# The last projection of the second row block by seven half-size products, with weight sums read back from memory

## The chip, the cores and the metric

One Trainium2 chip, one core. The time is the device time of one execution in microseconds; of a kernel that runs several times the median is given. Its five queues work side by side: TensorE (matmuls, PE in the profile), VectorE (DVE), ScalarE (ACT), GpSimd (POOL) and the sync queue (SP), which only issues DMAs. All DMAs share 16 engines.

## The reference

Two sequences of 512 and 1024 rows with 1024 columns pass through one layer: a mixer (attention and gated linear attention) and then an MLP, each added to its input, and a last norm. The change is in the MLP alone; all is float32.

```python
D_FF = -(-8 * D_MODEL // (3 * 256)) * 256        # 2816
def swiglu(hn, w_gate, w_up, w_down):
    return (jax.nn.silu(hn @ w_gate) * (hn @ w_up)) @ w_down
...
    x = x + swiglu(rmsnorm(x, norm2_g[l]), w_gate[l], w_up[l], w_down[l])
return rmsnorm(x, final_norm_g)
```

## The kernel before

The mixer's result goes to memory (`x2d`). The MLP then takes the 1536 rows as two blocks of 768 rows (`Block`, 6 tiles of 128 rows), and for each block all 2816 inner columns in 11 groups of 256 (`Group`; `NG` is 11). A product of two float32 matrices is made of three matmuls: each operand is split into a high part and the rest (`split`: ScalarE casts the high part, VectorE subtracts), and high x high, high x rest and rest x high are added in PSUM.

Gate and up are made with Winograd's form of Strassen's scheme. A block's normed rows, transposed, are cut in quarters (upper and lower half of the 1024 inner indices, even and odd tiles of rows), and from them seven forms (`FORMS`, b11 to b22, t1 to t4) are kept for the whole block, high and rest (`self.B`). A group's 1024 x 256 weights are cut in quarters as well, and `Weights.prepare(n)` makes seven sums of them, one for each product n, with four additions on VectorE, and splits each into a tile cw (pools `wc`, 5 buffers, and `hx`, 2). `Group.product(wn, n)` then multiplies cw with form n: 4 x 3 matmuls of 384 columns (L1075) into a PSUM tile gu; `common` combines the seven results (L1080, L1083). `w_gate` applies silu, `w_up` multiplies and splits the factor into g.

`Group.down(i)` multiplies g with the rows of `w_down` of the group (tile wd, L84 to L86) in the plain way: for each of 6 row tiles and each half of the 1024 output columns 2 x 3 matmuls of 512 columns, then an addition on VectorE into the result `xa` (L1142). After the last group `final` norms the rows and stores them.

The list `units` sets the order of a group: seven gate products, the down steps of the group before it, seven up products. `raw` loads the weights of one group, 1 MB a load, on the sync queue (tile rw or rd, pool `wr`, 2 buffers); `prepare_to` makes weights four products ahead of their use in the source. The framework then orders each engine's instructions by itself, by what is ready. During block 0, groups 3, 5 and 7, `blocks[1].rows` and `blocks[1].turn` norm and transpose the rows of block 1; `put` splits each form into a wc tile (f) and stores both halves in memory (`formd`), and `Block.fetch` loads them while block 0 ends. `blocks[1].residual` loads block 1's rows into `xa` at its first gate product.

Of the kernel before, what the change touches and what calls it, by code (L numbers as in the profile page):

```python
# [8 lines left out]
F32 = mybir.dt.float32  # L9
F32R = mybir.dt.float32r  # L10
# [33 lines left out]
def tile_trunk(ctx: ExitStack, tc: tile.TileContext, a: dict):  # L44
# [7 lines left out]
    FORMS = ("b11", "t2", "b21", "t3", "t1", "t4", "b22")  # L52
    formd = {x: [dram.tile([P, 4, 384], F32, name=f"{x}{w}_d") for w in "hl"] for x in FORMS}

# [819 lines left out]
    if True:  # L874
# [5 lines left out]
        g2 = cf.tile([P, D], F32, name="g2")  # L880
# [8 lines left out]
        class Block:  # L889
# [35 lines left out]
            def turn(self, q, tr_p, tag):  # L925
# [21 lines left out]
                sub = lambda o, i0, i1: nc.vector.tensor_tensor(out=o, in0=i0, in1=i1, op=ALU.subtract)  # L947

# [4 lines left out]
                def b11():  # L953
                    tr = quarter(0, 0)
                    sub(t[1], t[3], tr)
                    put("b11", tr)
# [7 lines left out]
                def t1():  # L964
                    put("t1", t[1])
                    sub(t[1], t[2], t[1])

                def b21():
                    put("t2", t[1])
                    tr = quarter(1, 0)  # L970
                    sub(t[1], tr, t[1])
                    put("b21", tr)
# [30 lines left out]
        wr_p = pool(left, "wr", 2, side="left")  # L1003
        wc_p = pool(left, "wc", 5, side="left")
        wd_p = pool(left, "wd", 2, side="left")
        g_p = pool(left, "g", 1, side="left")
        e_p = pool(left, "e", 7, side="left")
# [5 lines left out]
        raws = {}  # L1013

        def raw(blk, grp, wn):

            if wn == "w_down":
                wt = wr_p.tile([P, 2, D], F32, tag="wr", name=f"rd{blk}{grp}")
                src = a[wn][0, grp * 256:(grp + 1) * 256, :].rearrange("(n p) c -> p n c", p=P)
            else:  # L1020
                wt = wr_p.tile([P, KD, 256], F32, tag="wr", name=f"r{wn}{blk}{grp}")
                src = a[wn][0, :, grp * 256:(grp + 1) * 256].rearrange("(k p) c -> p k c", p=P)
            nc.sync.dma_start(out=wt, in_=src)
            raws[blk, grp, wn] = wt

        class Weights:


            def __init__(self, blk, grp, wn):
                self.key, self.nm = (blk, grp, wn), f"{wn}{blk}{grp}"  # L1030
                self.w = {}

            def prepare(self, n):
                r = raws[self.key]
                a11, a12, a21, a22 = [r[:, KH * k:KH * k + KH, P * f:P * f + P] for f in range(2) for k in range(2)]
                tt = lambda o, i0, i1, op: nc.vector.tensor_tensor(out=o, in0=i0, in1=i1, op=op)
                if n == 1:
                    self.s1, self.s2 = [sm_p.tile([P, KH, P], F32, tag="sm", name=f"{x}{self.nm}") for x in ("s1", "s2")]
                    tt(self.s1, a21, a22, ALU.add)
                    tt(self.s2, self.s1, a11, ALU.subtract)  # L1040
                elif n == 3:
                    tt(a21, a11, a21, ALU.subtract)
                elif n == 6:
                    tt(a12, a12, self.s2, ALU.subtract)
                src = [a11, None, a12, a21, None, a22, a12][n]
                src = self.s2 if n == 1 else self.s1 if n == 4 else src
                own, tag = (hx_p, "hx") if n in (2, 5) else (wc_p, "wc")
                wc = own.tile([P, 2, KH, P], F32R, tag=tag, name=f"c{self.nm}{n}")
                split(wc[:, 0], wc[:, 1], src)
                self.w[n] = wc  # L1050
# [274 lines left out]
```

## Time and profile before

| | us |
|---|---|
| median of 3 runs | 1954.68 (1954.45 to 1959.6) |
| the profiled execution | 1959.88 |
| its span, first to last instruction | 1958.1 |
| busy: TensorE, VectorE, ScalarE, GpSimd | 1917.9, 1377.4, 849.4, 80.5 |
| the MLP's first product starts at | 926.9 |

In the profile PE is TensorE's matmuls and PEld its weight loads, L with a number is a line of the kernel, out<-in are the tiles by the program's names with buffer numbers left out (dn, gu: PSUM tiles; cw: split weights; g: split factors; wd: split rows of w_down; xa: result rows). Matmuls overlap: a matmul's busy time is longer than the step from its start to the next one's. PEclk is the clock that TensorE was granted, as a share of 2.4 GHz. A row of waits says who waited, for what, how long in total, how often, and the longest.

### The profile page before, as it was taken

The numbers are of one execution on the slowest core, as the hardware profiler recorded it, in microseconds if no ns is written. First come the engines' busy times: TensorE is split into PE (matmuls) and PEld (weight loads), VectorE is DVE, ScalarE is ACT, GpSimd is POOL, SyncE is SP. The second block draws the span as 40 slices with busy tenths as digits, with TensorE's granted clock in tenths as the row PEclk, the third lists the DMA queues.
The fourth block names the chain that finished last, engine by engine and source line by source line (L and its number), as shares of the span: only waits on it lengthen the run. The fifth ranks groups of instructions, "written<-read, shape, count | busy, mean of one in ns | idle before, by whom it ended". The sixth has DMA issues, their size and how long they took to land.

```text
span 1958.1 us, 32024 instructions
## 1 busy us (share of the span) xinstructions
PE 1917.9 (98%) x12212; PEld 1769.5 (90%) x12212; DVE 1377.4 (70%) x3158; ACT 849.4 (43%) x2018; POOL 80.5 (4%) x113
## 2 busy tenths in 40 slices
PE   7999999999999999999999999999999999999997
PEld 7888889899998888999999999999998999999997
DVE  5677765737567777554777878797767777777775
ACT  5565555646445455332433434343343333333333
POOL 0110001110000000000000000000020000000001
PEclk9999999999998999999999999999999999999999
DMA  5233230202312233364421425152382222211211
GB/s 141 60 89 90 61 94 20 60 15 59 88 32 77 73 101 96 122 199 139 161 81 65 146 81 162 65 163 85 118 344 86 65 65 78 73 65 65 80 51 65
DMA packets 173642, 185.16 MB, mean 95 GB/s; under 512 B 16752, under 2 KB 149936, under 8 KB 173488
## 3 DMA queue, kind: packets, MB, share of 16 engines
q1 hardware_dynamic: 173488, 183.12, 29.6%
q8 instruction: 96, 1.57, 0.3%
q14 instruction: 58, 0.48, 0.1%
HBM read 151.03 MB, written 32.05 MB: 93 GB/s over the span
## 4 chain that ended last, share of the span: by engine, by line
PE 87%; DVE 4%; DMA 4%; ACT 2%; issue 1%; POOL 1%; SPq 0%; POOLq 0%; DVEq 0%; ACTq 0%
PE gu L1075 32%; PE acc L84 6%; PE acc L86 6%; PE dn L85 6%; PE acc L85 6%; PE dn L86 6%; PE dn L84 6%; PE sc L302 3%; PE pv L402 2%; PE trp L379 2%; PE acco L84 2%; PE acco L85 2%; PE acco L86 2%; PE kv L643 2%; DMA wr_ata<-w_in 1%
## 5 line engine op out<-in xcount | busy, mean ns | idle before, releaser
L1142 DVE TENSOR_TENSOR xa<-dn,xa 128x512 f32<-128x512 f32 x264 | 178.9, 688 | 88.0 <-PE dn L86 86.9
L84 PE MATMUL dn<-wd,g 128*128 128x512 f32 x528 | 205.8, 390 | 2.9 <-ACT wd L70 2.9
L85 PE MATMUL dn<-wd,g 128*128 128x512 f32 x528 | 206.2, 391 | 0.5 <-DVE wd L71 0.5
L86 PE MATMUL dn<-wd,g 128*128 128x512 f32 x528 | 206.0, 390 | 0.0
L70 ACT CAST wd<-rd 128x1024 fp32r<-128x1024 f32 x44 | 44.0, 1047 | 239.6 <-PE dn L86 239.6
L1080 DVE TENSOR_TENSOR u<-gu,u 128x384 f32<-128x384 f32 x176 | 97.3, 553 | 55.0 <-PE gu L1075 54.5
L70 ACT CAST cw_gate<-rw_gate 128x512 fp32r<-128x512 f32 x110 | 67.9, 621 | 125.5 <-PE gu L1075 83.6
L84 PEld LDWEIGHTS dn<-wd,g 128*128 128x128 f32 x528 | 99.2, 188 | 23.0 <-ACT wd L70 3.3
L85 PEld LDWEIGHTS dn<-wd,g 128*128 128x128 f32 x528 | 99.3, 188 | 20.7 <-DVE wd L71 1.2
L86 PEld LDWEIGHTS dn<-wd,g 128*128 128x128 f32 x528 | 99.4, 188 | 20.3
L358 ACT ACTIVATE sm<-sm,st 128x256 f32<-128x256 f32 (+1 forms) x160 | 86.7, 543 | 60.5 <-DVE st L352 60.3
L70 ACT CAST cw_up<-rw_up 128x512 fp32r<-128x512 f32 x110 | 67.7, 620 | 89.7 <-PE gu L1075 43.2
L71 DVE TENSOR_TENSOR cw_up<-rw_up,cw_up 128x512 fp32r<-128x512 f32 x110 | 75.3, 688 | 26.9 <-ACT cw_up L70 25.1
L84 PE MATMUL acc<-w_atb,hnh_b 128*128 128x384 f32 x256 | 91.3, 357 | 0.0
L86 PE MATMUL acc<-w_atb,hnl_b 128*128 128x384 f32 x256 | 88.0, 344 | 0.0
L85 PE MATMUL acc<-w_atb,hnh_b 128*128 128x384 f32 x256 | 87.8, 343 | 0.0
L71 DVE TENSOR_TENSOR cw_gate<-rw_gate,cw_gate 128x512 fp32r<-128x512 f32 x110 | 75.1, 684 | 7.2 <-ACT cw_gate L70 6.8
L379 PE MATMUL trp<-ident,sm 128*128 128x128 f32 x384 | 61.7, 286 | 1.2 <-DVE hnl_b L71 0.7
L347 DVE CUSTOM_DVE_ANT_0 sm<-sc,mask_b 128x256 f32<-128x256 f32 x128 | 49.9, 417 | 17.7 <-PE trqk L254 9.0
L86 PE MATMUL acco<-wo,ml_b 128*128 128x384 f32 (+1 forms) x192 | 61.5, 320 | 0.0
L84 PE MATMUL acco<-wo,mh_b 128*128 128x384 f32 (+1 forms) x192 | 61.3, 319 | 0.0
L85 PE MATMUL acco<-wo,mh_b 128*128 128x384 f32 (+1 forms) x192 | 61.0, 318 | 0.0
(414 smaller groups left out, 5742.0 us busy)
## 6 DMA issues: line engine op xcount, KB each, us to landing
rw_gate<-w_gate SPq DMA_DIRECT2D x22, 1024.0 KB, 5.3
rd<-w_down SPq DMA_DIRECT2D x22, 1024.0 KB, 5.0
rw_up<-w_up SPq DMA_DIRECT2D x22, 1024.0 KB, 5.4
wr_ata<-w_in SPq DMA_DIRECT2D x32, 192.0 KB, 2.5
wr_atb<-w_in SPq DMA_DIRECT2D x32, 192.0 KB, 2.6
wt<-lsed SPq DMA_DIRECT2D x32, 128.0 KB, 3.3
mr_b<-mixd_b SPq DMA_DIRECT2D x8, 512.0 KB, 4.5
xr_b<-x_sample SPq DMA_DIRECT2D x8, 512.0 KB, 4.0
```

The costliest lines, as they stand in the source:

```text
L70: nc.scalar.copy(out=h, in_=src)
L71: nc.vector.tensor_tensor(out=l, in0=src, in1=h.bitcast(F32), op=ALU.subtract)
L84: nc.tensor.matmul(out, xh, wh, start=(k == 0), stop=False)
L85: nc.tensor.matmul(out, xh, wl, start=False, stop=False)
L86: nc.tensor.matmul(out, xl, wh, start=False, stop=(k == n - 1))
L302: nc.tensor.matmul(outs[hd], lhs(x[b:b + 64]), rhs(y[b:b + 64]), start=(n == 0), stop=(n == 2))
L347: nc.vector.tensor_tensor_reduce(out=sm[:, cs], in0=sc[:, cs], in1=mks[g], scale=1.0, scalar=-3e38, op0=ALU.add, op1=ALU.max, accum_out=st ...
L358: nc.scalar.activation(out=sm[:, cs], in_=sm[:, cs], func=AF.Exp, scale=0.125, bias=st[:, NM, pat, hd, i0 + g:i0 + g + 1], accum_out=st[:, ...
L379: nc.tensor.transpose(tr[:, i], sm[:, i * P:(i + 1) * P], ident)
L1075: nc.tensor.matmul(ps, wc[:, wp, k], src[:, k], start=(own == n and k == 0 and i == 0), stop=(k == KH - 1 and i == 2), skip_group_check=True)
L1080: add = lambda o, i0: nc.vector.tensor_tensor(out=o, in0=ps, in1=i0, op=ALU.add)
L1142: nc.vector.tensor_tensor(out=acc[i][:, cs], in0=ps, in1=acc[i][:, cs], op=ALU.add)
```

## The change

Block 1's down projection takes groups in pairs and is made by the same seven-product scheme: the left quarters are even and odd row tiles by first and second half of the inner columns (group columns are now 128 from each half of the 2816), the right ones the halves of `w_down`'s rows and columns. The 21 steps (7 products, 3 pairs of row tiles each) stand between the seven gate products of the next group. Three products share a PSUM chain: a result is added to `xa` after each, and the next product goes on in the same bank. Group 10 of block 1 and all of block 0 stay plain.

The sums of weights are made once. Block 0 makes those of gate and up as before and stores them in memory (`summed`, four tiles per weight and group); those of `w_down` are made in memory by DMAs, plain copies issued by ScalarE and accumulating ones issued by GpSimd (`strips`), one after about every second product of groups 1 to 9. Block 1 reads quarters and sums back. All loads are now tiles of 128 x 512 (256 KB), through 6 `wr` buffers of that size; `wc` has 4 buffers instead of 5. Signs of some forms change (m1, m2 for t1, t2). `blocks[1].residual` moves from block 1's first gate product to its first up product, the load of `final_norm_g` from the start to block 0's last group, and block 0's last row is scaled like the others.

```diff
+            out[c] += [(copy, sm[x], qu[y]) for x, y in ((1, (0, 0)), (3, (0, 1)), (2, (1, 1)), (4, (1, 0)))]
+            out[c + 1] += [(add, sm[1], qu[0, 1]), (add, sm[3], qu[1, 1])]
+            out[c + 2] += [(add, sm[2], sm[1])]
+            out[c + 3] += [(add, sm[4], sm[2])]
...
-        wr_p = pool(left, "wr", 2, side="left")
-        wc_p = pool(left, "wc", 5, side="left")
-        wd_p = pool(left, "wd", 2, side="left")
-        g_p = pool(left, "g", 1, side="left")
-        e_p = pool(left, "e", 7, side="left")
+        wr_p = pool(left, "wr", 6, side="left")
+        wc_p = pool(left, "wc", 4, side="left")
+        wd_p = pool(left, "wd", 4, side="left")
+        gf_p = pool(left, "gf", 4, side="left")
+        e_p = pool(left, "e", 15, side="left")
...
+            def summed(self, wn, n):
...
+                if n == 1:
+                    for x in (1, 2):
+                        self.r[wn, x] = sm_p.tile([P, 512], F32, tag="sm", name=f"s{x}{wn}{self.grp}")
+                    add(self.r[wn, 1], q(1, 0), q(1, 1))
+                    add(self.r[wn, 2], self.r[wn, 1], q(0, 0))
+                    add(q(1, 0), q(0, 0), q(1, 0))
+                    self.r[wn, 3] = q(1, 0)
+                    for x in (1, 2, 3):
+                        put(x)
...
+            def left(self, n):
...
+                a11, a12, a21, a22 = [self.e[x] for x in ((0, 0), (1, 0), (0, 1), (1, 1))]
+                if n == 1:
+                    self.s1, self.s2 = self.tmp("s1"), self.tmp("s2")
+                    sub(self.s1, a22, a21)
+                    neg(self.s2, self.s1, a11)
+                elif n == 2:
+                    sub(a21, a11, a21)
+                elif n == 5:
+                    neg(self.s2, self.s2, a12)
+                src = a11 if n == 0 else self.s2 if n in (1, 5) else (a21, a22, self.s1)[n - 2] if n < 5 else a12
+                self.w["left", n] = self.factor(f"f{n}_", src)
...
+        def down(blk, grps, n, q):
+            acc, gs = blocks[blk].acc, [groups[blk, x] for x in grps]
+            fresh = n in (0, 4, 6)
+            if fresh:
+                chain[q] = dn_p.tile([P, 512], F32, tag="dn", name="dn")
+            ps = chain[q]
+            ts = slice(q * P, q * P + P)
+            for i, g in enumerate(gs):
+                x, w = g.w["left", n], g.w["w_down", n]
+                for m, (xp, wp) in enumerate(((0, 0), (0, 1), (1, 0))):
+                    nc.tensor.matmul(ps, x[:, xp, ts], w[:, wp], start=(fresh and i == 0 and m == 0),
+                                     stop=(i + 1 == len(gs) and m == 2), skip_group_check=True)
+            t, c, op = ((0, 0, ALU.add), (0, 1, ALU.subtract), (1, 1, ALU.subtract), (1, 0, ALU.add),
+                        (1, 1, ALU.subtract), (0, 1, ALU.subtract), (0, 0, ALU.add))[n]
+            o = acc[2 * q + t][:, 512 * c:512 * c + 512]
+            nc.vector.tensor_tensor(out=o, in0=o, in1=ps, op=op)
...
-                if key == (1, 0) and wn == "w_gate" and n == 0:
+                if key == (1, 0) and wn == "w_up" and n == 0:
                     blocks[1].residual()
...
+                if key[0] == 0 and 0 < key[1] < NG - 1:
+                    at = 14 * (key[1] - 1) + n + (7 if wn == "w_up" else 0) + 1
+                    while strip and (total - len(strip)) * 14 * (NG - 2) < at * total:
+                        f, o, x = strip.pop(0)
+                        x = f(o, x)
+                        tc.add_manual_dep(
+                            getattr(x, "ins", x), ins.name,
+                            mybir.DependencyInfo(mybir.DependencyClass.Sync, mybir.DependencyReason.DATA), reason="pace",
+                        )
```

## Rows read from the trace of the kernel before

**Rows 1.** The page: busy us, share of the span and instructions, by engine.

```profile
PE 1917.9 (98%) x12212; PEld 1769.5 (90%) x12212; DVE 1377.4 (70%) x3158; ACT 849.4 (43%) x2018; POOL 80.5 (4%) x113
```

**Rows 2.** TensorE's waits, 860 to 1940 us: total, times, longest.

```profile
PE gu L1075 <- ACT cw_gate L70: 3.4, 1, 3.4
PE dn L84 <- ACT wd L70: 2.9, 1, 2.9
PE gu L1075 <- ACT cw_up L70: 1.7, 1, 1.7
```

**Rows 3.** Windows: bounds, length, busy us of each engine, PEclk, DMA share, GB/s.

```profile
920.00:1430.00 510.00, 504.72 (x2680) 472.35 (x2679) 394.25 (x648) 192.38 (x338) 5.67 (x8) 1.00 0.37 122
1420.00:1440.00 20.00, 20.00 (x94) 17.01 (x93) 15.51 (x32) 12.17 (x30) 7.33 (x8) 1.00 1.03 404
1470.00:1476.00 6.00, 3.38 (x9) 2.50 (x10) 5.02 (x7) 3.96 (x6) 0.00 (x0) 0.72 0.05 5
1476.00:1482.00 6.00, 6.00 (x26) 5.86 (x25) 4.46 (x8) 2.23 (x4) 0.00 (x0) 0.71 0.49 169
1520.00:1566.00 46.00, 46.00 (x245) 43.19 (x244) 34.01 (x56) 15.37 (x28) 0.00 (x0) 1.00 0.22 69
```

**Rows 4.** Timeline of TensorE: start, duration, line, tiles.

```profile
1423.21 0.39 PE L84 MATMUL dn<-wd,g 128*128 128x512 f32 x1
...
1423.89 0.39 PE L84 MATMUL dn<-wd,g 128*128 128x512 f32 x1
...
1445.44 0.34 PE L1075 MATMUL gu<-t3h,cw_gate 128*128 128x384 f32 x1
...
1447.52 0.34 PE L1075 MATMUL gu<-t1h,cw_gate 128*128 128x384 f32 x1
```

**Rows 5.** Timeline of the sync queue: DMA issues.

```profile
924.87 2.06 SPq L922 DMA_DIRECT2D xa<-x2d_a  x4
...
1537.67 0.37 SPq L1023 DMA_DIRECT2D rw_gate<-w_gate  x1
...
1583.23 0.37 SPq L1023 DMA_DIRECT2D rw_gate<-w_gate  x1
```

**Rows 6.** Groups by line: busy us, mean ns, idle before.

```profile
L1142 DVE TENSOR_TENSOR xa<-dn,xa 128x512 f32<-128x512 f32 x264 | 178.9, 688 | 88.0 <-PE dn L86 86.9
L1080 DVE TENSOR_TENSOR u<-gu,u 128x384 f32<-128x384 f32 x176 | 97.3, 553 | 55.0 <-PE gu L1075 54.5 <-issue 0.5
L70 ACT CAST cw_up<-rw_up 128x512 fp32r<-128x512 f32 x110 | 67.7, 620 | 89.7 <-PE gu L1075 43.2 <-DVE rw_up L1036 24.2 <-PE dn L86 13.4
```

**Rows 7.** Timeline of VectorE in the old down step of block 1.

```profile
1541.69 0.69 DVE L1142 TENSOR_TENSOR xa<-dn,xa 128x512 f32<-128x512 f32 x1 [0.67 <-PE dn L86]
1543.02 0.69 DVE L1036 TENSOR_TENSOR s1w_gate<-rw_gate 128x512 f32<-128x512 f32 x1 [0.64 <-DMA rw_gate<-w_gate]
1543.63 0.68 DVE L1142 TENSOR_TENSOR xa<-dn,xa 128x512 f32<-128x512 f32 x1
1544.23 0.68 DVE L1036 TENSOR_TENSOR s2w_gate<-s1w_gate,rw_gate 128x512 f32<-128x512 f32 x1
...
1566.23 0.56 DVE L71 TENSOR_TENSOR g<-u,g 128x384 fp32r<-128x384 f32 x1
1566.70 0.55 DVE L1121 TENSOR_TENSOR c<-c,c 128x384 f32<-128x384 f32 x1
```

**Rows 8.** DMA issues by line: count, KB each, median us to landing.

```profile
rw_gate<-w_gate SPq DMA_DIRECT2D x22, 1024.0 KB, 5.3
x_b<-x_sample SPq DMA_DIRECT2D x14, 256.0 KB, 2.7
xa<-x2d_a SPq DMA_DIRECT2D x4, 512.0 KB, 9.3
t1l_d<-ft SPq DMA_DIRECT2D x3, 256.0 KB, 5.4
t4h<-t4h_d SPq DMA_DIRECT2D x1, 768.0 KB, 16.8
```

## What the change will do to the time

> **What bounds the kernel now.** I read the page first. TensorE is busy 98% of the span, against 70% for VectorE, 43% for ScalarE and 4% for GpSimd [rows 1]. A busy share is an average, so next come the idle times of the two MLP blocks: in the whole of both blocks TensorE waits at only eight places, and the three largest, 3.4, 2.9 and 1.7 us, are the first weights of block 0 and the first down tile of block 1; the rest are under 1 us [rows 2]. The windows say the same: over 46 us of block 1 TensorE is busy 46.00 us at granted clock 1.00, while the DMA engines are at a share of 0.22 [rows 3]. So a matmul that is taken out of block 1 should come out of the time, if nothing new makes TensorE wait.
>
> Then the price of one matmul, from start to start, since their busy times overlap. A down product of 512 columns takes three steps in 0.68 us, 227 ns each; twelve gate or up products of 384 columns take 2.08 us, 173 ns each [rows 4]. A group of block 1 has 14 x 12 of the small and 72 of the large ones: 14 x 2.085 + 72 x 0.2273 = 45.55 us. The sync queue issues the load of rw_gate at the same place 45.56 us apart [rows 5]. TensorE's sum alone is thus the period of a group, with nothing over.
>
> **The change part by part.**
> *The matmuls.* Block 1 pairs its groups 0 to 9; group 10 stays plain. For a pair, the old form has 2 x 72 = 144 down matmuls; the new one has 7 products x 3 row blocks x 2 groups x 3 split terms = 126. That is 18 fewer in each of 5 pairs, 90 in all: 90 x 0.2273 = **-20.5 us**. A pair takes 87.0 us instead of 91.1. I take the same 227 ns, since the shapes of the operands stay.
>
> *VectorE in the down phase.* The 21 steps of a pair's down now lie between the 7 gate products of the next group: 14.6 + 28.6 = 43.2 us of TensorE. VectorE has to do, beside them, 7 weight splits, 14 splits of w_down tiles and 21 additions to the result, 42 of 512 columns, and 14 splits of left factors, 8 sums for these and 5 gate additions, 27 of 384. Durations are 688 and 553 ns [rows 6], but back to back the start-to-start time is 0.60 and 0.47 [rows 7]. That gives 42 x 0.60 + 27 x 0.47 = 37.9 us by steps, or 43.8 us by durations. The steps are what a full queue pays, so I take 37.9, 88% of the phase. In the other 43.8 us of the pair it has less: with the sums of gate and up weights (8 per group) gone, 7 x 0.60 + 5 x 0.47 per gate and 4 x 0.47 more per up. Each factor of step n+1 may be made once step n-1 has left its buffers (four of each kind, two per step): from there to its use are two gate products and one down step, 2.09 + 4.09 + 2.09 = 8.3 us, in which VectorE owes some 7 us, the additions of the running step among them. The same bank may be added to again after two other row blocks and a gate product, 4.8 us after its last matmul, for one addition of 0.60. Queued behind a factor that waits are these additions, and TensorE waits for them; the cover is 1 to 4 us a step. That the engines' order is not the order of the source helps: s1w_gate stands between additions of an older group, so preparing work moves up into holes [rows 7]. Cost 0 to 0.6 us per phase, 0 to 3 in all, if VectorE does not wait at the wrong place (a rival, below).
>
> *ScalarE.* Per phase 21 casts of 512, 14 of 384, a copy and silus: with 0.62 us for all [rows 6] some 25 of 43 us. Nothing.
>
> *Finer loads.* Loads of 1 MB become loads of 256 KB, the gate and up ones in rows of 512 B instead of 1 KB; block 1 reads 7 tiles instead of 4 for each weight. A pair reads 42 tiles, 11 MB in 87 us, 127 GB/s, against 404 GB/s that a saturated stretch moved [rows 3]. Loads of 256 KB land in 2.7 us [rows 8], and six buffers run ahead. Nothing in block 1.
>
> *First loads.* Block 0's first product waits for a whole 1 MB load, 5.3 us; it will wait for 256 KB, 2.7 us [rows 2, 8]. The second product needs two tiles more and two sums. Bounds 0 and -5.1 (both waits); I take **-2.5**, the difference of the landings.
>
> *The entry of block 1.* Its first down tile is late because the queue is behind form loads and stores, and TensorE then runs at clock 0.72 and 0.71 for 12 us: 9 + 26 matmuls where a steady stretch has 32 + 32 [rows 3], 29 x 0.188 = 5.4 us. The new first down comes two groups later, so this wait goes. What is late next are the finer gate tiles, behind the forms at a DMA share of 1.03 [rows 3]. The residual's six loads move from the first gate product to the first up product and help here; they are needed 30 us later. Bounds 0 and -5.4; I take **-3.5**.
>
> *Block 0's own additions.* It stores 8 sums per group, 23 MB in all, on the sync queue. Strips of w_down sums are made in memory: 32 copies issued by ScalarE, 32 accumulating ones by GpSimd, 11.5 MB each kind. DMA load: 23 MB at 404 GB/s are 57 us, the copies 29, the accumulating ones 29 if they cost one pass and 87 if three (no row shows one), and 23 MB in half as long rows 0 to 57. Together 115 to 230 us on top of a share of 0.37 of 510 us [rows 3]: 0.59 to 0.82. I take 0.65. Each strip waits for a product to end; behind it in ScalarE's queue are casts, and in GpSimd's the power for row norms, both needed many microseconds later. An issue takes 0.37 us [rows 5], so without cover 32 x 0.37 = 12 us; the six weight tiles made ahead (12 us of products) hide it. The turns of block 1's rows get four wc buffers instead of five (a rival, below). final_norm_g is loaded late instead of first, and block 0's last row is scaled by ScalarE and GpSimd as the others: nothing. For the turns, the strips and the down phases together I take **+3**, from 0 to 8.
>
> *Sum.* -20.5 - 2.5 - 3.5 + 3 = -23.5 us. The profiled execution took 1959.9 (span 1958.1 and 1.8 around it), 5.2 above the median of the runs shown, 1954.7; it would become 1936.4, and the median **1931**. Bounds: -31.0 is 1924, -20.5 + 8 is 1942.
>
> **The rivals.**
> *VectorE takes TensorE's place in the down phases.* For: 88% by steps, 101% by durations, and in the old down it idles 0.67 us before most additions, as it waits at the head of its queue [rows 7]. If it does that before each of 21, the phase has 37.9 + 14.1 = 52.0 us, 8.8 more than TensorE needs, 44 us in five phases: 1975. Halfway it is 22 us: about 1953. Against: the old down had little else to do in those holes.
>
> *Form tiles run out of buffers, slower than before.* Place: block 0, the three turns. Each turn writes 7 form tiles through the wc buffers and stores them; a buffer is held for a split (1.2 us) and until the store has landed. A turn takes some 10 products, 20.9 us, in which 7 weight tiles hold a buffer at least 3.3 us each, 23 us. Four buffers give 84 us, so a form may hold 8.7, a store may take 7.5. Such stores of 256 KB now take up to 5.4 us; under a saturated queue loads took 9.3 and 16.8 [rows 8]. Past 12 us a store, a turn takes 4 x 29 us, three turns lose 24 us and the gain is gone; at 16.8 us 7 x 18 + 23 is 149, 37 us a turn, 3 x 16.5 = 50 lost: 1931 + 50 = 1981. It decides at a DMA share near 1 in block 0; my sum says at most 0.82.
>
> *Loads one after another.* If each 256 KB load went alone, a pair needed 42 x 2.7 = 113 us instead of 87: 5 x 26 = 132 us, some 2060. Against: the queue issued four loads of rows within 2.06 us [rows 5]; with two in flight it is 57 us. The Trainium skill's page DMA: Bandwidth & Descriptors, section Bandwidth, says to batch to at least 1 MiB and speaks against this change; the fit in its section Anatomy of one DMA gives 2.6 us for 256 KB, an estimate, which would make 109 us a pair. The 2.7 us of the row agrees; what decides is the number in flight.
>
> **How the numbers follow.** Forecast (1922 to 1943) 0.70; VectorE (1942 to 1975) 0.14; buffers (1942 to 1981) 0.11; single loads 0.03; anything else 0.02. The range 1922 to 1954 holds 0.68 of the forecast, 0.09 of VectorE's case and 0.03 of the buffers'. A measurement of this kernel tells 0.3% (5.9 us) from no change: faster is below 1948.8, slower above 1960.5. Faster: 0.70 + 0.06 of VectorE's case + 0.01 = 0.77. Within: 0.05 of VectorE's, 0.02 of the buffers' and 0.01, 0.08. Slower: 0.03 + 0.09 + 0.03 = 0.15.
>
> **What would show it.** 90 matmuls fewer (12212 to 12122); a pair of groups 87.0 us from gate to gate, 57.8 for the even one with the down steps and 29.2 for the odd one; TensorE waits under 0.5 us a step in the down phases; VectorE there 85 to 90% busy by steps; no slow clock at the entry of block 1; DMA share of block 0 between 0.59 and 0.82, form stores under 7.5 us. I am wrong on the main term if TensorE waits for xa or f at each step, and on block 0 if cw tiles are waited for in groups 3, 5 and 7.

## The result, and the profile after

The changed kernel takes **1972.3 us** (median of 6, 1969.6 to 1977.8) against 1957.9 for the kernel before on the same chip: a ratio of 1.0082, 95% interval 1.0064 to 1.0099. It is slower, where I forecast 1931 and a range that ended at 1954. Its profiled execution has a span of 1970.2 us, 12.1 more than the 1958.1 of before.

The page of the kernel after: engines (as [rows 1]), then the DMA queues with packets, MB and share of 16 engines.

```profile
PE 1910.6 (97%) x12122; PEld 1753.8 (89%) x12122; DVE 1365.6 (69%) x3198; ACT 885.1 (45%) x2123; POOL 109.4 (6%) x146
...
q1 hardware_dynamic: 245248, 231.38, 37.9%
q0 software_dynamic: 6144, 11.54, 4.0%
q10 hardware_dynamic: 6144, 11.54, 2.0%
```

The 90 matmuls are gone (12212 to 12122). Loads and stores of the sync queue are on q1, GpSimd's accumulating strips on q0, ScalarE's copies on q10. Windows of the kernel after (columns as [rows 3]): the stretch of block 0 that [rows 3] has as first row, the 57 us in which the first turn ends, one pair of block 1, and the entry of block 1.

```profile
920.00:1430.00 510.00, 480.39 (x2466) 440.03 (x2466) 363.82 (x618) 179.43 (x332) 32.16 (x38) 0.98 0.70 195
...
1093.00:1150.00 57.00, 52.09 (x263) 47.52 (x262) 44.14 (x77) 20.38 (x39) 2.67 (x4) 0.97 0.86 233
1508.30:1595.30 87.00, 87.00 (x463) 82.00 (x462) 66.15 (x114) 36.96 (x69) 0.00 (x0) 1.00 0.45 134
...
1460.00:1490.00 30.00, 28.86 (x143) 25.55 (x143) 22.11 (x45) 17.42 (x40) 11.51 (x12) 1.00 0.98 388
```

In block 1 TensorE waits for nothing: it is busy 87.00 of 87.00 us. In the first row TensorE is idle for 29.6 us; in the same stretch before it was 5.3 [rows 3], nearly all of it ahead of the first product. To place the loss I took from each trace's timeline of TensorE the time between the first matmuls of the last up product (b22 with cw_up) of successive groups; "group 3" is the interval that ends in group 3.

| | groups 1, 2 | 3 | 4 | 5 | 6 | 7 | 8 | 9, 10 | sum |
|---|---|---|---|---|---|---|---|---|---|
| before | 45.6, 45.6 | 48.2 | 44.9 | 48.2 | 44.9 | 48.2 | 44.9 | 45.6, 45.6 | 461.7 |
| after | 47.7, 47.2 | 49.4 | 52.2 | 54.8 | 53.9 | 55.7 | 53.7 | 47.6, 45.6 | 507.8 |

So block 0 is **46.1 us** longer, 40 of them in groups 3 to 8, where the three turns lie (each begins in the up products of group 3, 5 or 7 and ends in the next group). The other differences: the first product of block 0 starts at 920.7 instead of 926.9 (-6.2, of which 2.7 are the mixer, whose last matmul ends at 920.8 instead of 923.5); the two intervals at the entry of block 1 are 76.3 us, 1.5 over a steady 45.6 + 29.2, where before they were 99.6, 8.4 over 2 x 45.6 (-6.9); the matmuls give -20.5. Together +12.5, against the 12.1 of the spans.

Of the 46 us, 31.1 are 23 long steps from one matmul to the next, and 16.3 are 126 steps that are at least 40 ns over the steady 173 or 227 ns and at most some 2.8 times as long (worked out from the timeline). Of these 16.3, some 9.5 us lie in six stretches, 20.4 us together, in which the granted clock was 0.50; the rest are short waits. The waits of TensorE and ScalarE in block 0 after, 958 to 1452 us (total, times, longest):

```profile
PE gu L1116 <- ACT u L1126: 8.4, 3, 4.4
PE gu L1116 <- ACT cw_gate L96: 6.8, 4, 2.9
PE gu L1116 <- DVE u L1123: 4.2, 6, 1.1
PE gu L1116 <- DVE cw_gate L97: 3.5, 3, 1.3
...
ACT wd L96 <- DMA rw_down<-w_down: 43.1, 18, 4.0
...
ACT ft L96 <- DMA b22l_d<-fb: 12.4, 3, 4.7
...
ACT junk L940 <- DMA hx<-x2d_b: 10.8, 6, 5.3
```

TensorE waits for ScalarE and VectorE, but they are not the limit (45% and 69%): ScalarE stands at the head of its queue for a raw tile, for a form store to free its buffer, for the rows of a turn. The longest case step by step, from the timelines of the kernel after (ScalarE; the sync queue; VectorE; GpSimd; TensorE):

```profile
1259.46 0.62 ACT L96 CAST cw_gate<-s1w_gate 128x512 fp32r<-128x512 f32 x1
1265.38 1.06 ACT L940 ACTIVATE junk<-hx 128x1024 bf16<-128x1024 f32 x1 [5.31 <-DMA hx<-x2d_b]
...
1266.84 0.47 ACT L1126 COPY u<-gu 128x384 f32<-128x384 f32 x1
...
1257.37 0.51 SPq L937 DMA_DIRECT2D hx<-x2d_b  x1
...
1266.56 0.15 DVE L89 TENSOR_SCALAR ms_n<-ss 128x1 f32<-128x1 f32 x1 [4.88 <-ACT junk L940]
...
1256.77 0.86 POOL L74 DMA_DIRECT2D w_downs<-w_downs  x1 [4.25 <-PE gu L1116]
1261.18 0.86 POOL L74 DMA_DIRECT2D w_downs<-w_down  x1 [3.55 <-PE gu L1116]
...
1267.36 0.44 PE L1116 MATMUL gu<-b21h,cw_gate 128*128 128x384 f32 x1 [4.40 <-ACT u L1126]
```

The hx rows of the turn are asked for at 1257.37, between two accumulating strips, and land 8 us later. ScalarE stands 5.31 us at the square of hx; behind it in its queue is the copy of u, and TensorE waits 4.40 us for that. Over the 6 us after the wait TensorE's granted clock is 0.72 on average: it is at 1.2 GHz (0.50) for a part of them and at 2.4 GHz for the rest:

```profile
1267.40:1273.40 6.00, 6.00 (x26) 6.00 (x27) 4.13 (x7) 1.96 (x4) 0.93 (x2) 0.72 0.21 48
...
1267.73:1271.13 3.40, 3.40 (x13) 3.40 (x12) 3.15 (x5) 0.61 (x2) 0.00 (x0) 0.50 0.00 0
...
1273.40:1280.00 6.60, 6.60 (x39) 6.51 (x38) 2.01 (x4) 1.05 (x2) 0.00 (x0) 1.00 0.82 206
...
1102.40:1108.40 6.00, 5.01 (x18) 4.55 (x19) 5.64 (x10) 3.03 (x7) 0.00 (x0) 0.72 1.06 310
```

26 matmuls where a steady 6 us has 35 of this kind: 1.5 us more for a wait of 4.4. The same 0.72 follows the waits at 1102 (the last row), 1157 and 1219 us.

### The profile page after: what moved, and what is told of

The parts are those of the page before. It is cut to its first block, busy times and chain, and to the rows that moved or that the text cites. A ratio compares the mean times of both kernels' runs of the same rounds, so it can differ in the third digit from the quotient of the medians.

```text
span 1970.2 us, 33156 instructions
## 1 busy us (share of the span) xinstructions
PE 1910.6 (97%) x12122; PEld 1753.8 (89%) x12122; DVE 1365.6 (69%) x3198; ACT 885.1 (45%) x2123; POOL 109.4 (6%) x146
## 4 chain that ended last, share of the span: by engine, by line
PE 75%; DMA 10%; DVE 8%; ACT 3%; issue 2%; POOL 1%; SPq 1%; POOLq 0%; DVEq 0%; ACTq 0%
PE gu L1116 23%; PE dn L1228 7%; PE acc L110 7%; PE acc L112 6%; PE acc L111 6%; PE sc L328 3%; PE pv L428 3%; PE trp L405 2%; DMA rw_down<-w_down 2%; PE dn L110 2%; PE dn L112 2%; PE dn L111 2%; PE kv L669 2%; PE acco L110 2%; PE acco L111 1%
## 5 line engine op out<-in xcount | busy, mean ns | idle before, releaser
L1228 PE MATMUL dn<-cw_down,f 128*128 128x512 f32 x630 | 148.9, 390 | 0.0
L1228 PEld LDWEIGHTS dn<-cw_down,f 128*128 128x128 f32 x630 | 117.8, 188 | 22.3
L110 PE MATMUL dn<-wd,g 128*128 128x512 f32 x288 | 113.8, 395 | 2.3 <-DVE xa L1207 2.0
L97 DVE TENSOR_TENSOR cw_up<-rw_up,cw_up 128x512 fp32r<-128x512 f32 x132 | 90.9, 693 | 34.1 <-ACT cw_up L96 30.9
L112 PE MATMUL dn<-wd,g 128*128 128x512 f32 x288 | 112.4, 390 | 0.0
L1207 DVE TENSOR_TENSOR xa<-dn,xa 128x512 f32<-128x512 f32 x144 | 95.9, 687 | 23.6 <-PE dn L112 22.3
L111 PE MATMUL dn<-wd,g 128*128 128x512 f32 x288 | 112.2, 390 | 0.0
L96 ACT CAST wd<-rw_down 128x512 fp32r<-128x512 f32 x48 | 29.8, 621 | 153.1 <-PE dn L112 100.9
L1233 DVE TENSOR_TENSOR xa<-xa,dn 128x512 f32<-128x512 f32 x105 | 71.9, 685 | 13.9 <-PE dn L1228 12.0
L110 PEld LDWEIGHTS dn<-wd,g 128*128 128x128 f32 x288 | 54.1, 188 | 16.3 <-DVE xa L1207 5.7
L96 ACT CAST cw_down<-rw_down 128x512 fp32r<-128x512 f32 x70 | 43.4, 619 | 53.6 <-PE dn L1228 22.4
L112 PEld LDWEIGHTS dn<-wd,g 128*128 128x128 f32 x288 | 54.1, 188 | 11.2 <-DVE g L97 0.3
L111 PEld LDWEIGHTS dn<-wd,g 128*128 128x128 f32 x288 | 54.1, 188 | 10.2
L97 DVE TENSOR_TENSOR wd<-rw_down,wd 128x512 fp32r<-128x512 f32 x48 | 33.1, 689 | 42.8 <-ACT wd L96 42.8
```

The source lines that it names most:

```text
L96: nc.scalar.copy(out=h, in_=src)
L97: nc.vector.tensor_tensor(out=l, in0=src, in1=h.bitcast(F32), op=ALU.subtract)
L110: nc.tensor.matmul(out, xh, wh, start=(k == 0), stop=False)
L111: nc.tensor.matmul(out, xh, wl, start=False, stop=False)
L112: nc.tensor.matmul(out, xl, wh, start=False, stop=(k == n - 1))
L1207: nc.vector.tensor_tensor(out=acc[i][:, cs], in0=ps, in1=acc[i][:, cs], op=ALU.add)
```

## The experiments

My theory after the result: the traffic for the weight sums, and in it the strips, makes block 0's loads and stores land late. The rivals: the sum stores; the wc buffers, four instead of five; any traffic of that size. Times are medians; ratios are to runs of the kernel before on the same chip, in brackets their 95% interval; "block 0" is the sum of the ten intervals above (461.7 before, 507.8 after), from the one profiled execution of each run. The end of the mixer differs between such executions by up to 8 us (918.1 to 926.2 us in the sixteen whose mixer is that of the kernel after), so a difference of a few us between two such executions, or between two medians of four runs, is weak. Where sums are left out (e2 to e6, e17, e18) the result is not the layer's, and only the time is read; e2, e3, e4, e17 and e18 load other tiles of the same size in place of the missing sums.

### Which part of the change

```diff
 e1_wc5
-        wc_p = pool(left, "wc", 4, side="left")
+        wc_p = pool(left, "wc", 5, side="left")
-        e_p = pool(left, "e", 15, side="left")
+        e_p = pool(left, "e", 12, side="left")
 e2_nostrips
...
-        strip = strips()
+        strip = []
 e3_nostores
...
-                    for x in (1, 2, 3):
-                        put(x)
...
-                    nc.sync.dma_start(out=sums[wn][4][self.grp], in_=a12)
 e4_neither: e2 and e3
```

> The changed kernel with five wc buffers instead of four, as before the change; the room for it is taken from the e tiles (12 instead of 15), which only block 1 can feel. Block 1's pairs took 87.0 us as forecast and block 0 took some 45 us more than before, 38 of them in groups 4 to 8, during and after the turns. Theory of buffers (form tiles hold wc buffers until late stores have landed, so weight tiles are made late): groups 4 to 8 lose less than 15 us in place of 38, and the time falls by 20 to 30 us, to about 1947. Theory of traffic (every DMA is late, and ScalarE and VectorE wait in their queues for loads): under 8 us of gain, 1964 or more.

> No strips: the 64 DMAs that make the sums of w_down in memory are left out, with their issues on ScalarE and GpSimd and their waits; block 1 reads a quarter of w_down in place of each sum, same size, so its down projection is not the reference's. The strips' queues take 21 points of the DMA share in block 0. Theory of traffic: the share in the turn groups falls from 0.80-0.86 to 0.6-0.65, form stores land in 3 to 4 us instead of 6 to 7, block 0 gets back 20 to 35 us, 1940 to 1952. Theory of buffers: a turn still loses the fifth buffer, and block 0 gets back 5 to 15 us, 1957 to 1967.

> No stores of the gate and up sums in block 0 (88 DMAs, 23 MB, on the sync queue); block 1 reads other 128 x 512 pieces of the weights with 2 KB rows in their place, so block 1's result is not the reference's. Theory of traffic: as many bytes as the strips, but cheaper for the DMA engines (57 us of share against 115), so 10 to 20 us back, 1952 to 1962. If what counts is the sync queue, where loads stand behind stores that wait for VectorE, then more than without strips: 20 to 35 us back, and the ordinary groups 1, 2 and 9 lose under 1 us instead of 2. Theory of buffers: 5 us or less.

> Neither strips nor stores, as in the two kernels before, so block 1's result is not the reference's. What is left in block 0 of the change are the finer loads, six small buffers for them and four wc buffers. Theory of traffic: nearly all of the 45 us come back, about 1928 to 1935, which is also what I forecast for the whole change. Theory of buffers or of the finer loads: block 0 still loses 15 us or more, 1943 or above.

Measured: e1 1959.8, 1.0019 [1.0007, 1.0031]; e2 1940.8, 0.9924 [0.9908, 0.9940]; e3 1966.3, 1.0049 [1.0032, 1.0066]; e4 1937.1, 0.9900 [0.9885, 0.9915]. Block 0: 493.5, 476.0, 504.2, 471.7. So the strips cost **31.5 us**, the stores of the gate and up sums, which move about as many bytes, 6 (3.7 once the strips are gone, e4 against e2), and the fifth wc buffer is worth 12.5 while the strips run. The 31.5 are what traffic was expected to give; the 6 are less than its 10 to 20, and the 12.5 lie between my two theories of e1. With both out, block 0 is still 10 us longer than before, and the time lies above the 1928 to 1935 expected from traffic alone.

Neither the mean share of the DMA engines nor the time of a weight load tells these apart. Windows of e2 and e3 over the same stretch:

```profile
958.00:1452.00 494.00, 484.71 (x2527) 444.65 (x2525) 371.26 (x636) 182.85 (x345) 13.28 (x16) 1.00 0.51 163
```

```profile
958.00:1452.00 494.00, 465.18 (x2391) 425.75 (x2391) 347.97 (x588) 166.08 (x307) 32.05 (x38) 0.99 0.56 145
```

e3 has a share of 0.56 and moves less than e2 (145 against 163 GB/s), and TensorE is busy 19.5 us less. (The last 23 us of e2's window are the entry of block 1 already; within block 0 alone it has 0.48 and 151 GB/s, e3 0.56 and 146.) Issues from 950 to 1460 us, count, KB, median us to landing: first the kernel after, then e2, then e3. The median goes over the transfers whose landing the trace shows, of gate and up loads 7 and 22 in the kernel after, 13 and 15 in e2, 16 and 11 in e3.

```profile
rw_up<-w_up SPq DMA_DIRECT2D x42, 256.0 KB, 5.2
...
rw_gate<-w_gate SPq DMA_DIRECT2D x39, 256.0 KB, 5.8
...
m2h_d<-fm SPq DMA_DIRECT2D x3, 256.0 KB, 6.8
```

```profile
rw_up<-w_up SPq DMA_DIRECT2D x43, 256.0 KB, 3.2
...
rw_gate<-w_gate SPq DMA_DIRECT2D x41, 256.0 KB, 3.2
...
t3h_d<-ft SPq DMA_DIRECT2D x3, 256.0 KB, 3.4
```

```profile
rw_gate<-w_gate SPq DMA_DIRECT2D x43, 256.0 KB, 3.9
rw_up<-w_up SPq DMA_DIRECT2D x41, 256.0 KB, 3.9
...
t3h_d<-ft SPq DMA_DIRECT2D x3, 256.0 KB, 4.7
```

With strips and stores a gate or up load takes 5.2 to 5.8 us, with stores alone 3.2. But with strips alone (e3) it takes 3.9, and block 0 keeps nearly all of its loss; so the time of these loads is not the measure of it. The stores of the turns' forms tell more: over all form stores with a landing in the trace (10 to 24 of 42 in a run) the median is 4.2 to 5.4 us in the seven runs with strips in the turns, 2.9 to 3.3 in the other thirteen. And the mean share hides how it is spread. Cut into pieces of 2 us, the stretch from group 0's last up product to group 9's has 164 us at a DMA share of 0.95 or more in the kernel after, 112 in e3, 58 in e2 and 58 before; e5 and e14, whose mean share there (0.55 and 0.53) is near e3's 0.56 and which lose far less, have 70 and 82 (worked out from the traces). These two go along with the loss; no run sets them by themselves.

The Trainium skill, page DMA: Bandwidth & Descriptors, section Queues, rings and completion order, says that each DMA engine goes round-robin between its queues, a packet at a time. No run here tests it: stores that stand in the loads' own queue cost 6 us and strips on two other queues 31.5, but the strips also go from memory to memory, and half of them add. The runs don't show the order of single packets either.

### Which part of the strips

e5 leaves out the 32 accumulating transfers and keeps the 32 copies; e6 makes the 32 plain copies; e12 cuts them into pieces of 512 bytes.

```diff
 e5_copies
-            out[c + 1] += [(add, sm[1], qu[0, 1]), (add, sm[3], qu[1, 1])]
-            out[c + 2] += [(add, sm[2], sm[1])]
-            out[c + 3] += [(add, sm[4], sm[2])]
 e6_plainadds
-            ... nc.gpsimd.dma_start(out=o[r], in_=i[r], accum_op=ALU.add, max_dma_last_dim=2048)
+            ... nc.gpsimd.dma_start(out=o[r], in_=i[r], max_dma_last_dim=2048)
 e12_small
+            ... nc.gpsimd.dma_start(out=o[r], in_=i[r], accum_op=ALU.add, max_dma_last_dim=512)
```

> Half of the strips: the 32 accumulating DMAs from GpSimd are left out, the 32 plain copies from ScalarE with their waits stay (so the sums are not complete and block 1's result is not the reference's). Without strips 32 us came back. Theory of packets (an accumulating packet of 2 KB holds a DMA engine 178 to 220 ns where a copy holds it 84 to 109 and a 512 B load packet 28, so loads and stores that share the engines with it land 2 to 3 us later): 20 to 28 us back, 1944 to 1952. Theory of waits (ScalarE, which stands before a strip until a product has ended, makes casts and PSUM copies late): under 8 us back, 1964 or more.

> All 64 strips stay, from the same queues, at the same places, with the same waits and bytes, but GpSimd's 32 do not accumulate: they are plain copies over the sum (so the sums are wrong and block 1's result is not the reference's). Theory of packets: a packet holds its engine half as long, so about half of the accumulating strips' part comes back, 8 to 15 us, 1957 to 1964. Theory of waits, or of the number of DMAs in flight: nothing changes, 1970 to 1974.

> The changed kernel with the accumulating transfers cut into pieces of 512 bytes instead of 2048, same bytes, same places. Theory one, a load's small packets wait behind single long ones (178 ns against 28): with four short ones in place of each the loads land as early as without strips and the time falls by some 15 to 25 us, to about 1950. Theory two, it is the engines' time that the additions take: pieces of 512 bytes take it up at least as long, 1972 or more, up to some 2000 if each piece costs the same 178 ns.

Measured: e5 1946.4, 0.9931 [0.9913, 0.9949]; e6 1959.6, 0.9999 [0.9982, 1.0016]; e12 1974.7, 1.0094 [1.0062, 1.0125]. ScalarE's copies cost 5.6 us by the medians (e5 against e2; 1.4 by the ratios, whose intervals overlap), GpSimd's transfers 26, about half of it because they accumulate (e6: 12.7 less than after). GpSimd's queue q0, 950 to 1460 us, packets, MB and share, in the kernel after (with ScalarE's copies, q10, below it), in e6 and in e12:

```profile
q0 software_dynamic: 6144, 11.54, 15.3%
q10 hardware_dynamic: 6144, 11.54, 7.6%
```

```profile
q0 software_dynamic: 3584, 11.54, 7.7%
```

```profile
q0 software_dynamic: 23040, 11.54, 19.7%
```

The same 11.5 MB take the engines twice as long when they are added instead of copied. Smaller pieces take longer still and bring nothing: theory one of e12 (short packets between the loads' own) falls. Theory two, that the engines' time is what costs, is not shown by it: the share of q0 rises from 15.3% to 19.7%, and the time of e12 is that of the kernel after within the noise.

### Where the strips run

e7 moves all strips into the mixer ahead of the MLP; e8 has five wc buffers besides. e9 puts 16 of them in groups 1 and 2, 16 in groups 9 and 10, 32 in the first seven groups of block 1, so that none meets a turn; e10 has five wc buffers besides.

```diff
 e7_mixer (in the mixer's loop over its steps)
+        strip = strips()
...
         for i, f in enumerate(steps):
             f()
+            while strip and ... :
+                g, o, x = strip.pop(0)
...
 e9_spread
...
-        strip = strips()
+        strip = {"A": strips(0, 2), "B": strips(2, 2), "C": strips(4, 4)}
...
-                if key[0] == 0 and 0 < key[1] < NG - 1:
...
+                at = n + (7 if wn == "w_up" else 0) + 1
+                part, at, width = (
+                    ("C", 14 * key[1] + at, 96) if key[0] else
+                    ("A", 14 * (key[1] - 1) + at, 28) if key[1] in (1, 2) else
+                    ("B", 14 * (key[1] - 9) + at, 28) if key[1] > 8 else (None, 0, 1)
+                )
...
```

> The strips moved: all 64 are issued during the mixer (between a tenth and nine tenths of its steps, each after a matmul of its step), where the DMA share is 0.2 to 0.3, and none in block 0. Everything is computed. If what they cost is their meeting with block 0's loads and stores, block 0 is as without strips, and the time is that of the kernel without them, 1941, plus what the mixer loses, 0 to 8 us. If it is the strips' own work, wherever they stand, the mixer grows by 20 us or more and the time stays above 1960.

> The strips in the mixer and five wc buffers (12 e tiles). Without strips block 0 still took 14 us more than before, in and after the turns. If that is the fifth buffer, 8 to 12 us of it come back against the strips in the mixer with four: about 1931 if the mixer loses nothing, and faster than both kernels. If it is the stores and the finer loads, within 4 us of the run with four buffers.

> The same 64 transfers for the sums of w_down, none of them in groups 3 to 8, where the turns are: 16 in groups 1 and 2 of block 0, 16 in groups 9 and 10, 32 in the first seven groups of block 1, each before the pair that reads it. Theory one, they cost only where they meet a turn (loads and stores of the turn land late, ScalarE and VectorE stand behind them in their own order): the intervals of groups 3 to 8 become those of the kernel without the transfers (51, 46.5, 50, 47.6, 51, 46), all others keep 45.6 in block 0 and 29.2 and 57.8 in block 1: about 1943. Theory two, they cost wherever TensorE is saturated, some 0.5 us each as now: the loss moves into groups 9 and 10 and into block 1, pairs grow from 87.0 to some 91, about 1970.

> As the run before, with five wc buffers instead of four and twelve e buffers instead of fifteen. In the changed kernel the fifth buffer was worth 12.5 us; if four buffers are short by themselves, groups 4, 6 and 8 keep 46 and groups 3, 5 and 7 fall from 51 to the 48 of the old kernel: 9 us less than the run before, about 1934. If four were short only because the transfers made loads and stores late, there is nothing left to gain: equal to the run before within 3 us.

Measured: e7 1980.5, 1.0103 [1.0081, 1.0124]; e8 1967.9, 1.0048 [1.0034, 1.0061]; e9 1964.3, 1.0039 [1.0022, 1.0056]; e10 1953.8, 0.9971 [0.9952, 0.9990]. In e7 block 0 falls to 474.4, as without strips, but its first product starts at 960.7 instead of 920.7: the mixer pays 40 us. In e9 the turns are cured (groups 3 to 8 294.7, e2 292.1, after 319.7), and the loss turns up elsewhere: groups 1, 2 and 9 are 48.1, 49.7 and 49.9, the entry 84.9 instead of 76.3, of which 5.7 are the first odd group of block 1; the other pairs lose 0.7 together. Both theories of e9 hold in part: the turns are not the only place, but after its first odd group block 1 takes the same strips for almost nothing. In e10 the fifth buffer is worth 10.5 us, as the first theory of e10 had it, from a higher start. TensorE's largest waits in e9 are for VectorE's addition to a gate or up product (11.3 us in 7 places), no longer for a turn.

### Buffers

```diff
 e11_before_wc4 (the kernel before)
-        wc_p = pool(left, "wc", 5, side="left")
+        wc_p = pool(left, "wc", 4, side="left")
 e13_wr8 (the kernel after)
-        wr_p = pool(left, "wr", 6, side="left")
+        wr_p = pool(left, "wr", 8, side="left")
...
-        e_p = pool(left, "e", 15, side="left")
+        e_p = pool(left, "e", 12, side="left")
...
-        room = 6
+        room = 8
 e17_nostrips_wr8: e2 and e13
 e18_nostrips_wc5: e2 and e1
```

> The kernel before with four wc buffers instead of five, nothing else. If the fifth buffer is needed by the turns whatever else runs, groups 3, 5 and 7 grow from 48.2 to about 51 and the time by 8 to 10 us, to about 1967. If it is short only under late stores, nothing: 1958.

> The changed kernel with eight buffers for raw weight tiles instead of six, so that loads are issued two tiles further ahead (twelve e buffers instead of fifteen make the room); the transfers of the w_down sums stay as they are. Theory one, the loads of weights are issued too late to bear 2 to 3 us more on the way: two tiles more are about two products, 4 us, which covers it; what stays are the waits on hx loads and form stores of the turns: about 1955. Theory two, the loss lies in the turns' own loads and stores, which stop ScalarE and VectorE: 1968 to 1972.

> Left out: the transfers that make the w_down sums; block 1 reads quarters of w_down in their place (same bytes). With eight raw buffers and twelve e buffers. If six raw buffers are short in block 0 without any strip, as e16 against e14 suggests, the time falls from 1940.8 (six buffers) to 1931 or less, and the VectorE sums of e16 cost nothing beside it. If the 15 us of e16 came only from holding raw tiles for the sums, six were enough here: 1940.

> Left out: the same transfers. With five wc buffers instead of four, twelve e buffers, six raw buffers. The fifth wc buffer was worth 10 to 12 us wherever strips ran and in the kernel before, 2 us with the sums on VectorE. If the turns need it by themselves: about 1931. If what they lacked was a wc buffer only when raw tiles come late: 1938 to 1941.

Measured: e11 1967.3, 1.0056 [1.0036, 1.0076]; e13 1962.4, 1.0024 [1.0009, 1.0039]; e17 1931.5, 0.9860 [0.9843, 0.9876]; e18 1936.6, 0.9879 [0.9861, 0.9896]. The fifth wc buffer has its worth in the old kernel already: 10 us, 5.9 of them in block 0. Without strips, two more raw buffers bring 9.3 us by the medians (12.5 by the ratios), the fifth wc buffer 4.2 (8.8 by the ratios); block 0 goes from 476.0 to 468.3 and 469.1. So either of them gives back some 7 us of block 0, about as much as e4 could not place. A raw tile is free once it is split into wc, so I take it that both lengthen one chain, the lead of a load; no run shows that by itself. With the strips the two raw buffers bring 10 of 41 us (1962.4 lies between the two theories of e13): TensorE's waits in e13, 958 to 1452 us, are those behind form stores and hx.

```profile
PE gu L1116 <- ACT cw_gate L96: 11.4, 5, 3.3
PE gu L1116 <- DVE u L1123: 4.0, 3, 2.5
PE gu L1116 <- ACT u L1126: 3.4, 2, 2.0
...
ACT cw_gate L96 <- DMA m1l_d<-fm: 8.4, 3, 3.8
...
ACT junk L940 <- DMA hx<-x2d_b: 8.2, 6, 3.4
```

### The same sums without strips

Each group of block 0 has the four quarters of its w_down rows in its buffers anyway. e14 lets VectorE add them in place after the splits, and the sync queue store them; e15 has five wc buffers besides (as e1), e16 eight raw buffers (as e13).

```diff
 e14_vsums (in rows; the order of the four tiles becomes 00, 01, 11, 10)
...
+                def add(x, o, i):
+                    nc.vector.tensor_tensor(out=q[o], in0=q[o], in1=q[i], op=ALU.add)
+                    nc.sync.dma_start(out=sums["w_down"][x][self.grp * P:self.grp * P + P], in_=q[o])
+                if (f, c) == (0, 1):
+                    add(1, (0, 0), (0, 1))
+                if (f, c) == (1, 1):
+                    add(3, (0, 1), (1, 1))
+                    add(2, (1, 1), (0, 0))
+                    return 2
+                if (f, c) == (1, 0):
+                    add(4, (1, 0), (1, 1))
+                    return 2
...
-        strip = strips()
+        strip = []
```

> The sums of w_down made by VectorE from the four tiles that each group of block 0 has loaded anyway, in place (four additions of 128x512 a group, 2.4 us of VectorE), and stored by the sync queue as the gate and up sums are (40 stores of 256 KB more); no transfer from memory to memory is left. 80 such stores for gate and up cost 6 us and the kernel without the transfers 1940.8, so 40 more cost 3 us: about 1944, clearly under the kernel before. Rival: the longer hold of two to four of the six raw buffers makes the next group's gate tiles late, 1 to 2 us a group: about 1958.

> As e14, with five wc buffers and twelve e buffers. The fifth buffer was worth 12.5 us in the changed kernel, 10 in the kernel before and 10 with the transfers spread: some 9 us under the run before this one, about 1935; if four suffice once the transfers are gone, equal to it.

> As e14, with eight raw buffers (and four wc, twelve e). If holding raw tiles for the sums is what costs there, it goes: down to about 1941. If not, equal to e14; the four wc buffers still cost the turns their 9 us.

Measured: e14 1946.8, 0.9942 [0.9920, 0.9965]; e15 1944.9, 0.9936 [0.9915, 0.9957]; e16 **1931.2, 0.9873 [0.9850, 0.9895]**, 41 us under the changed kernel and 27 under the one before. e16 equals e17, which doesn't make the sums at all: they cost nothing that the time shows (block 0 of the profiled executions is 471.1 against 468.3). The page's line of engines of e16, then a stretch that lies within block 0 in e3, e14 and e16, in this order, then TensorE's waits in e16 (958 to 1452 us):

```profile
PE 1893.6 (98%) x12122; PEld 1743.3 (90%) x12122; DVE 1389.9 (72%) x3238; ACT 888.6 (46%) x2123; POOL 81.3 (4%) x114
```

```profile
958.00:1370.00 412.00, 384.52 (x1975) 351.73 (x1975) 293.31 (x497) 141.13 (x262) 27.46 (x33) 0.98 0.57 149
...
958.00:1370.00 412.00, 399.66 (x2067) 365.03 (x2066) 327.44 (x557) 144.74 (x271) 4.24 (x6) 0.99 0.54 171
...
958.00:1370.00 412.00, 407.34 (x2132) 374.25 (x2131) 333.99 (x568) 153.02 (x278) 4.25 (x6) 1.00 0.54 172
```

```profile
PE dn L110 <- ACT g L96: 1.9, 2, 1.0
PE gu L1116 <- ACT e L1147: 1.3, 2, 1.0
PE gu L1116 <- ACT u L1126: 1.1, 1, 1.1
PE dn L110 <- DVE xa L1224: 0.9, 3, 0.3
```

At nearly e3's share (0.54 against 0.57) and with more bytes a second (171 against 149 GB/s) e14, with the same six raw buffers, has TensorE busy 399.66 us where e3 has 384.52, and e16 407.34. Traffic of that size is thus no loss in itself, and my third rival falls. My forecasts for e15 and e16 were each wrong by 10 us: I expected the gain from the fifth wc buffer, and it came from the raw buffers. That the raw tiles, held longer for the sums, are what is short in e14 and e15 is likely and not shown: eight buffers gain 16 us there, and 9 in e17, which has no sums.

## Why the prediction was wrong

*The matmuls* were right to the digit: 12122, a pair of 57.8 and 29.2, 87.0 together, -20.5 us. *VectorE in the down phases* and *ScalarE*, too: VectorE is busy 66.15 of 87.00 us of a pair, TensorE waits for nothing there, and the rival that had 0.14 is false. The measured time lies within its range (1942 to 1975), but only by coincidence. *Finer loads* cost nothing in block 1; the rival of single loads (0.03) is false.

*First loads* (-2.5) had about the right size: the wait of 3.4 us before the first product is gone, and the other 2.7 of the 6.2 us are the mixer's end, which differs that much from run to run. The reason was not the shorter landing: the first load is issued 10.3 us before the mixer's last matmul ends, where the 1 MB load, which waited 7.5 us in the sync queue for a matmul of the mixer, was issued 2.8 us before it (first the kernel before, then after):

```profile
920.68 0.38 SPq L1023 DMA_DIRECT2D rw_gate<-w_gate  x1
```

```profile
910.53 7.90 SPq L1065 DMA_DIRECT2D rw_gate<-w_gate  x4
```

*The entry* (-3.5) was too small, -6.9, beyond its bound of -5.4. The 12 us that I costed hold most of the wait of 2.9 us and the slow clock behind it; the intervals before have 8.4 us over a steady pace, since the start of that wait and shorter ones (0.6 and 0.3 us) stand ahead of those 12 us.

**Block 0's own additions is the step that failed**: +3, from 0 to 8, and it was 46.1. Its first half was right: I worked out a DMA share of 0.59 to 0.82 and took 0.65, and it is 0.70 in the same stretch. The sentence on cover was not: "the six weight tiles made ahead (12 us of products) hide it". I had set that cover against the time of an issue (0.37 us) and not against the time that every other transfer gets longer. The strips cost 31.5 us (e2). A form store takes 5.2 us with them instead of 3.3, a gate or up load 5.2 to 5.8 instead of 3.2, and the cover is not there for all: the rows of a turn, its form stores and the raw w_down tiles have their own lead, and ScalarE and VectorE wait for them in order, with the next product's casts and copies behind (5.31 us at the head of ScalarE's queue became 4.40 of TensorE). Behind six of TensorE's waits the granted clock was 0.50, which added some 9.5 us to the 31.1 of the long steps. I also took six raw buffers as ample, since in block 1 they are; in block 0 they cost 9 to 12 us even without strips (e2 against e17).

The terms close the miss: block 0 came out 43 us above its +3, the entry 3.4 and the first product 3.7 below theirs (2.7 of it the mixer), 36 in all; the spans moved by +12.1 where the sum had -23.5. Another 3 us lie in the base: three runs of the kernel before had a median of 1954.7, six have 1957.9.

*The rival of the form tiles* had the right place, the three turns, and 0.11 as its chance; its gauge was wrong. It was to decide at a DMA share near 1 and at stores past 7.5 us. The mean share is 0.70, 0.86 in the stretch of the first turn, the stores of m1 and m2 take 5.8 to 6.8 us, and 40 us are lost there nevertheless. In pieces of 2 us the share is near 1 for 164 us, nearly three times as long as before: a mean was the wrong gauge for it. I had counted one resource, the buffers of wc, as if all waits but a form's had cover; the fifth buffer gives back 12.5 of 41. What I had bounded by one pass or three, the accumulating strips, kept the engines twice as long as plain copies.

What stays open: how much of the strips' 31.5 us is the engines' time that they take, how much the way in which the queues take turns, and how much that they read and write memory at both ends. e6 halves the time of the accumulating queue and gives back 40% of the whole; e12 tells only that shorter pieces don't help. No run put the strips on the loads' own queue, and no run shows why e3, with loads of 3.9 us and 112 us near a share of 1, loses almost as much as the kernel after with 164.

## What to carry to other kernels

A transfer that nobody waits for is not free: ask how much later every other transfer on the same engines lands, and set that against the shortest lead among them, not against the longest cover; and look at the share in short stretches, not at its mean. Where an operand passes through the on-chip buffers anyway, make its sums there on an engine with room and store them; here, with the stores in the loads' own queue, that was 25 us cheaper than adding in memory (e14), 31 with eight raw buffers (e16 against e13). Check the number of buffers for each stage that shares a pool: six were enough in block 1, and in block 0 eight were 9 to 12 us better.

## What was not expected of the hardware

Accumulating transfers within memory took 15.3% of the time of 16 engines over 510 us for 11.5 MB, plain copies of the same bytes on the same queue 7.7%, the adding ones in pieces of 512 bytes 19.7%. Sixty-four transfers of 352 KB cost 40 us in the mixer, 31.5 in block 0, and some 6 to 9 for half of them at the entry of block 1 and in it.
